# Loads two chunks ahead, a third residual tile and tokens weighted in place in the stage of pooled product and backward states

## The chip, the cores and the metric

The kernel runs on one core of one Trainium2 chip. The metric is the device time of one execution in microseconds. Five engines work side by side, each through its own queue in order: PE (TensorE, matrix products; its loading of weights is listed as PEld), DVE (VectorE), ACT (ScalarE), POOL (GpSimd) and SP (SyncE, which here only issues DMAs; ACT issues the stores).

## The reference, cut to what matters

One layer of a diffusion trunk over 2048 latent tokens of width 1024, with 256 context tokens as a prefix:

```
x   = LN(x; emb_ln_g, emb_ln_b);  h = x * (1 + sc1) + sh1
z, xbc, dt, up = split(h @ in_proj);  xbc = silu(conv5(xbc))
y   = SSD forward + SSD backward over chunks of 128 tokens
      (16 heads x 64, state 128; the scans start from the context's states)
y   = rms_norm((y + d_skip * xs) * silu(z)) * ssd_norm_g
p   = pool_mixer(up): box means of windows 2, 4, 8, 16 minus the token,
      one 256x256 map for each of four groups, times pool_scale
mix = concat(y, p) @ w_out
x   = LN(alpha * x + g1 * mix);   x = LN(alpha * x + g2 * swiglu(modulate(x)))
```

The backward state runs from the last chunk to the first: `h = h * decay + B^T (x * w_end)` for each chunk. The state before each chunk is needed later, in the forward scan.

## The kernel before, in words

All is fp32. Large products are made of three matmuls on split operands: each operand is a rounded high part (fp32r, by a cast on ACT) and a low part (by a subtraction), and `mm3` (L71 and on) adds high x high, high x low and low x high in one PSUM tile. Matmuls have a moving side of 512 columns, and L72 is the line of every one of them.

The stages, in order: normalisation and projections with the convolution; scores and pooling, which write the pooled differences `dp_d` to memory; the z blocks together with `pooled_weights`, which folds the pool maps, the pool scale, the gate g1 and the lower half of `w_out` into one operand W2 (high and low, W2H and W2L); then the stage of this change; then the forward scan with the output projection; then the feed-forward layer, which is over half of the time.

The stage of this change goes from chunk c = 15 down to c = 0 (NCH = 16 chunks of P = 128 tokens). For each chunk it does three things.

- The pooled product: `dp_d` of the chunk (two halves `dl` of 128x512, split into `dh` by a cast at L1053 and `dl` by a subtraction at L1054) times W2, in two halves of 512 columns with 24 matmuls each.
- The residual: the row block `x` (tile `bx`) is loaded, normalised with the statistics `stat` kept from the first stage (L1067, on DVE), multiplied by `ag` and added to `ab` (L1068 and L1069, on POOL); the product is added to it from PSUM (L1086, DVE), and the sum is stored in `base_d`.
- The backward state (c > 0): the state `hb` is stored; the chunk's tokens `xt` (1024 columns of x and 128 of B) are loaded, x is weighted per head into a tile `xs` (L1062, POOL), and `add_state` (L368 and on) decays the state on DVE (L371), makes two matmuls of 512 columns, which are issued as two instructions each, and adds them (L377, DVE).

Beside this, one block of 128 rows of the upper half of `w_out` in every second chunk becomes the operand of the later output projection: two halves are loaded into one tile `wyraw`, multiplied by the norm's gain and g1 (L1096, DVE), cast into WyH (L1097, ACT) and subtracted into WyL (L1098, DVE).

`prep(c - 1)` does the loads and splits of the next chunk in the iteration of c, ahead of c's product. Tiles with a number in their tag (`dh0`, `dl1`, `bx0`, `xt1`) exist once for each parity of c (`dh` and `dl` in two halves each), so a load of chunk c - 2 waits until chunk c has done with the tile.

Two pools hold the tiles: `bp` at the left takes the place of two of the operands of the z blocks that ended earlier; `b3` at the right lies where other operands of the z blocks lay. `after(t)` writes one element of a tile on POOL from `gate`, which is ready when the third group of pooled weights is split, so that the load behind it does not stand in SP's queue too early.

The order of each engine's queue is laid out when the program is built, by a scheduler that follows the text's order only among instructions which its own model of time has ready at once. So a queue's order isn't the text's: all sixteen loads of `wyraw` are issued by 986 us, in the first nine chunks, where the text spreads them over fifteen. Waits within a queue are then in order: an instruction that waits holds up all that stand behind it on its engine.

Of the kernel before, what the change touches and what calls it, by code (L numbers as in the profile page):

```python
# [8 lines left out]
F32 = mybir.dt.float32  # L9
F32R = mybir.dt.float32r  # L10
I32 = mybir.dt.int32
AF = mybir.ActivationFunctionType
ALU = mybir.AluOpType

P = 128
D = 1024
KB = D // P
T = 2048
NCH = T // P
TC = 256  # L20
NCC = TC // P
H = 16
# [13 lines left out]
def hybrid_block_kernel(ctx: ExitStack, tc: tile.TileContext, a: dict, out: bass.AP, dbg=None):  # L36
    nc = tc.nc
    mult, add, sub, amin = ALU.mult, ALU.add, ALU.subtract, ALU.min
# [11 lines left out]
    def pool(name, side="left"):  # L50
        return tc.tile_pool(name=name, bufs=1, side=side, reuse_waits="tile")
# [10 lines left out]
    def load(dst, src):  # L62
        nc.sync.dma_start(dst, src)

    def store(dst, src):
        nc.scalar.dma_start(dst, src)

    def f32(ap):
        return ap.bitcast(F32)
# [4 lines left out]
    def mm3(ps, lh, ll, rh, rl, nk, tick=None):  # L74
        for k in range(nk):
            mm(ps, lh(k), rh(k), k == 0, False)
            mm(ps, lh(k), rl(k), False, False)
            mm(ps, ll(k), rh(k), False, k == nk - 1)
            if tick is not None:
                tick(k)  # L80
# [58 lines left out]
    xbc_d = dram.tile([T, D + P], F32, name="xbc_d")  # L139
    bt_d = dram.tile([P, T], F32, name="bt_d")  # L140
    ct_d = dram.tile([P, T], F32, name="ct_d")
    dp_d = dram.tile([D, T], F32, name="dp_d")
    sz_d = dram.tile([D, T], F32, name="sz_d")
    w_d = dram.tile([NCH, P, H * P], F32, name="w_d")
    base_d = dram.tile([T, D], F32, name="base_d")
    hb_d = dram.tile([NCH * P, D], F32, name="hb_d")
# [61 lines left out]
    stat = cst.tile([P, NCH, 2], F32, name="stat")  # L208
# [6 lines left out]
    def ln_h(src, t0, r, tp, parts, o, keep):  # L215

        st = small.tile([P, 2, 2, 6], F32, tag="st", name="st")
        mv = small.tile([P, 2, 2], F32, tag="mv", name="mv")
        ve = small.tile([P, 2], F32, tag="ve", name="ve")
        xs = []  # L220
        for i in range(2):
            x = tp.tile([P, D], F32, tag="lnx", name="lnx", bufs=6)
            if keep and t0 < 3 * 256:
                nc.gpsimd.tensor_copy(x[:, 0:1], mod_gate)
            load(x, src[t0 + i * P:t0 + (i + 1) * P, :])
            xs.append(x)
        yield
        for i in range(2):
            ln_stats(xs[i], st[:, i], mv[:, i])
        nc.vector.tensor_scalar(out=ve, in0=mv[:, :, 1], scalar1=EPS, scalar2=None, op0=add)  # L230
        rs = rsqrt(ve, 2, "rs")
        nm = small.tile([P, 2], F32, tag="nm", name="nm")
        nc.vector.tensor_scalar(out=nm, in0=mv[:, :, 0], scalar1=-1.0, scalar2=None, op0=mult)
        if keep:
            c0 = t0 // P
            nc.gpsimd.tensor_scalar(out=stat[:, c0:c0 + 2, 0], in0=nm, scalar1=1.0, scalar2=0.0, op0=mult, op1=add)
            nc.gpsimd.tensor_scalar(out=stat[:, c0:c0 + 2, 1], in0=rs, scalar1=1.0, scalar2=0.0, op0=mult, op1=add)
        for i in range(2):
            nc.gpsimd.tensor_scalar(out=xs[i], in0=xs[i], scalar1=nm[:, i:i + 1], scalar2=rs[:, i:i + 1], op0=add, op1=mult)
        yield  # L240
        w = slice(o, o + 256)
        HT, LT = parts()
        for k in range(KB):
            pt = ps_tr()
            for i in range(2):
                nc.tensor.transpose(pt[:, i * P:(i + 1) * P], xs[i][:, k * P:(k + 1) * P], ident)  # L246
            h = tp.tile([P, 256], F32, tag="h32", name="h32", bufs=3)
            if k % 4 == 1:
                nc.vector.tensor_scalar(out=h, in0=pt[:, 0:256], scalar1=modA[:, r, k:k + 1], scalar2=modB[:, r, k:k + 1], op0=mult, op1=add)
            else:  # L250
                nc.scalar.activation(out=h, in_=pt[:, 0:256], func=AF.Identity, scale=modA[:, r, k:k + 1], bias=modB[:, r, k:k + 1])
            nc.scalar.copy(HT[:, k, w], h)
            e = nc.vector if k % 4 == 3 else nc.gpsimd
            e.tensor_tensor(out=LT[:, k, w], in0=h, in1=f32(HT[:, k, w]), op=sub)
            yield
# [106 lines left out]
    def heads(ap):  # L362
        return ap.rearrange("p (h d) -> p h d", d=HD)

    def bch(ap, n=H, m=HD):
        return ap.unsqueeze(2).broadcast_to([P, n, m])

    def add_state(hn, hp, dec, xw, bt):  # L368

        if hp is not None:  # L370
            nc.vector.tensor_tensor(out=heads(hn), in0=heads(hp), in1=bch(dec), op=mult)  # L371
        for g in range(2):
            ps = ps_ss()
            s = slice(g * 512, (g + 1) * 512)
            mm(ps, bt, xw[:, s], True, True)
            if hp is not None:
                nc.vector.tensor_tensor(out=hn[:, s], in0=hn[:, s], in1=ps, op=add)  # L377
            else:
                nc.vector.tensor_copy(hn[:, s], ps)


    x_in = a["x"].rearrange("o t d -> (o t) d")
# [57 lines left out]
    class Ahead:  # L440

        gens = [None] * 8
        at, n = 0, 0
# [467 lines left out]
    w_out = a["w_out"].rearrange("o (k p) n -> p (o k) n", p=P)  # L911
# [105 lines left out]
    eac, wend, cdec = (coef[:, i] for i in range(3))  # L1017
# [10 lines left out]
    bp = sb.enter_context(pool("b2"))  # L1028
# [4 lines left out]
    def after(t):  # L1033
        nc.gpsimd.tensor_copy(t[:, 0:1], gate)
# [7 lines left out]
    hb = b3.tile([P, D], F32, tag="hb1", name="hb")  # L1042
    after(hb)
    load(hb, hb0)
    def prep(c):
        rows_c = slice(c * P, (c + 1) * P)
        dh, dl = [], []
        for q in range(2):
            dh.append((b3 if c % 2 else bp).tile([P, 4, P], F32R, tag=f"dh{c % 2}", name="dh", bufs=2))
            dl.append((b3 if c % 2 else bp).tile([P, 4, P], F32R, tag=f"dl{c % 2}", name="dl", bufs=2))  # L1050
            d = f32(dl[q])
            load(d, dp_d[q * 512:(q + 1) * 512, rows_c].rearrange("(k p) t -> p k t", p=P))
            nc.scalar.copy(dh[q], d)  # L1053
            nc.vector.tensor_tensor(out=dl[q], in0=d, in1=f32(dh[q]), op=sub)  # L1054
        xs = xt = None
        if c > 0:
            xt = b3.tile([P, D + P], F32, tag=f"xt{c % 2}", name="xt")
            if c >= NCH - 2:
                after(xt)
            load(xt, xbc_d[rows_c, :])  # L1060
            xs = b3.tile([P, D], F32, tag=f"xs{c % 2}", name="xs")
            nc.gpsimd.tensor_tensor(out=heads(xs), in0=heads(xt[:, 0:D]), in1=bch(wend[:, c, H:2 * H]), op=mult)  # L1062
        x = (b3 if c % 2 else bp).tile([P, D], F32, tag=f"bx{c % 2}", name="bx")
        if c >= NCH - 2:
            after(x)
        load(x, x_in[rows_c, :])
        nc.vector.tensor_scalar(out=x, in0=x, scalar1=stat[:, c, 0:1], scalar2=stat[:, c, 1:2], op0=add, op1=mult)  # L1067
        nc.gpsimd.tensor_tensor(out=x, in0=x, in1=ag, op=mult)  # L1068
        nc.gpsimd.tensor_tensor(out=x, in0=x, in1=ab, op=add)  # L1069
        return xs, xt, dh, dl, x  # L1070

    cur = prep(NCH - 1)
    for c in range(NCH - 1, -1, -1):
        rows_c = slice(c * P, (c + 1) * P)
        xs, xt, dh, dl, x = cur
        if c > 0:
            store(hb_d[rows_c, :], hb)
            hn = (b3 if c % 2 == 0 else sr).tile([P, D], F32, tag=f"hb{(c - 1) % 2}", name="hb")
            add_state(hn, hb, cdec[:, c, H:2 * H], xs, xt[:, D:D + P])
            hb = hn  # L1080
            cur = prep(c - 1)
        for nh in range(2):
            n = slice(nh * 512, (nh + 1) * 512)
            ps = ps_mm()
            mm3(ps, lambda k: dh[k // 4][:, k % 4, :], lambda k: dl[k // 4][:, k % 4, :], lambda k: W2H[k][:, n], lambda k: W2L[k][:, n], KB)
            nc.vector.tensor_tensor(out=x[:, n], in0=x[:, n], in1=ps, op=add)  # L1086
        store(base_d[rows_c, :], x)
        if c % 2 == 1:
            k = (NCH - 1 - c) // 2
            for nh in range(2):  # L1090
                n = slice(nh * 512, (nh + 1) * 512)
                raw = b3.tile([P, 512], F32, tag="wyraw", name="wyraw")
                if c == NCH - 1 and nh == 0:
                    after(raw)
                load(raw, w_out[:, k, n])
                nc.vector.scalar_tensor_tensor(out=raw, in0=raw, scalar=v_ng[:, k:k + 1], in1=g1b[:, n], op0=mult, op1=mult)  # L1096
                nc.scalar.copy(WyH[k][:, n], raw)  # L1097
                nc.vector.tensor_tensor(out=WyL[k][:, n], in0=raw, in1=f32(WyH[k][:, n]), op=sub)  # L1098
        if c == 1:
            bo.close()  # L1100
            se = sx.enter_context(pool("se", "right"))
    sb.close()
    ph1.close()

# [544 lines left out]
```

## Time and profile before

| | us |
|---|---|
| median of three runs | 2763.98 (2759.65 to 2764.54) |
| the profiled execution | 2764.45 |
| its span | 2762.7 |
| PE busy | 2649.9 (96%) |
| DVE busy | 1767.3 (64%) |
| POOL busy | 1371.5 (50%) |
| ACT busy | 913.3 (33%) |

Times in the trace count from the start of the span. Busy time is the time in which an engine had an instruction at work. Matmuls overlap in the profile, so the busy time of a group of matmuls is more than the time it takes; their pace is read from the chain of waits, where each piece begins where the one before ends. An arrow names what released a waiting instruction; where it waited for several things it names the last. Some matmul records are missing from a trace.

### The profile page before, as it was taken

The page shows a single profiled execution, that of the slowest core. Times are in us where ns is not written, and L with a number is a line of the kernel's source. Part 1 is how long each engine was busy: PE and PEld are TensorE (multiplying, and loading weights), DVE is VectorE, ACT ScalarE, POOL GpSimd, SP SyncE. Part 2 cuts the span into 40 slices and gives each one's busy share as a digit, 9 for nine tenths or more (in the row PEclk, how much of TensorE's full clock was granted, in tenths as well). Part 3 has the DMA queues.
Part 4 walks back from the last instruction along what each step waited for, and adds up shares of the span by engine and source line. Part 5 has one row for each costly group of instructions (what it writes and reads, how often), then busy time and mean ns, then how long its engine had stood idle before and what let it go on. Part 6 is the DMA issues. An engine that isn't in the chain of part 4 may idle for free.

```text
span 2762.7 us, 33705 instructions
## 1 busy us (share of the span) xinstructions
PE 2649.9 (96%) x11778; PEld 2053.4 (74%) x11778; DVE 1767.3 (64%) x2209; ACT 913.3 (33%) x1611; POOL 1371.5 (50%) x1166
## 2 busy tenths in 40 slices
PE   7989999999999899999989999999999998999997
PEld 4557788778877666777768888877888887888776
DVE  4748745864646675677786777777765555545763
ACT  3544332116532111343352332233323323333332
POOL 5654322433435454556554565555555543315467
PEclk9989999999999999999999999999999999999998
DMA  9822321226756566667664455564433327545643
GB/s 325 263 73 71 112 77 45 69 97 181 197 163 221 186 219 234 200 227 250 209 230 163 158 180 169 170 217 146 164 96 103 103 84 238 156 148 175 208 148 109
DMA packets 392449, 454.86 MB, mean 165 GB/s; under 512 B 31173, under 2 KB 287920, under 8 KB 388952
## 3 DMA queue, kind: packets, MB, share of 16 engines
q1 hardware_dynamic: 298016, 340.29, 39.7%
q10 hardware_dynamic: 93784, 112.30, 11.3%
q8 instruction: 93, 1.52, 0.2%
q0 software_dynamic: 480, 0.11, 0.1%
q14 instruction: 76, 0.62, 0.1%
HBM read 294.34 MB, written 158.28 MB: 164 GB/s over the span
## 4 chain that ended last, share of the span: by engine, by line
PE 80%; DMA 6%; DVE 5%; POOL 3%; issue 3%; ACT 2%; SPq 0%; ACTq 0%; POOLq 0%; DVEq 0%
PE b L72 42%; PE mm L72 30%; PE ss L72 6%; DVE cv L359 1%; DMA wada<-in_w_ada 1%; POOL acc L1530 1%; DMA base_d<-bx 1%; POOL acc L1529 1%; PE tr L1161 1%; PE tr L604 1%; PE tr L246 0%; DMA dl<-dp_d 0%; DMA lnx<-in_x 0%; DMA bx<-in_x 0%; PE tr L1211 0%
## 5 line engine op out<-in xcount | busy, mean ns | idle before, releaser
L72 PE MATMUL b<-wd,h 128*128 128x512 f32 x1848 | 433.9, 397 | 13.4 <-ACT h L1355 7.4
L72 PEld LDWEIGHTS b<-wd,h 128*128 128x128 f32 x1848 | 349.5, 190 | 97.6 <-DVE wd L1344 8.0
L72 PE MATMUL mm<-HT,wh 128*128 128x512 f32 x832 | 332.1, 402 | 2.8 <-ACT u L906 2.3
L72 PE MATMUL mm<-LT,wh 128*128 128x512 f32 x832 | 332.5, 400 | 0.0
L72 PE MATMUL mm<-HT,wl 128*128 128x512 f32 x832 | 331.1, 399 | 0.0
L1329 DVE TENSOR_TENSOR ev<-ev,b 128x512 f32<-128x512 f32 x301 | 200.8, 680 | 135.6 <-PE b L72 120.3
L1316 POOL TENSOR_TENSOR x<-cs,x 128x512 fp32r<-128x512 f32 x132 | 185.7, 1407 | 172.3 <-ACT x L1315 158.5
L1356 DVE TENSOR_TENSOR h<-h 128x768 fp32r<-128x768 f32 x112 | 125.8, 1131 | 155.0 <-ACT h L1355 154.8
L72 PEld LDWEIGHTS mm<-HT,wh 128*128 128x128 f32 x832 | 158.1, 190 | 40.2 <-ACT u L906 3.1
L72 PEld LDWEIGHTS mm<-LT,wh 128*128 128x128 f32 x832 | 157.6, 189 | 36.4 <-issue 0.6
L72 PEld LDWEIGHTS mm<-HT,wl 128*128 128x128 f32 x832 | 157.4, 189 | 36.5 <-issue 0.6
L359 DVE SCALAR_TENSOR_TENSOR cv<-raw,vt,cv 128x512 f32<-128x512 f32 (+2 forms) x160 | 134.0, 848 | 59.6 <-POOL cv L357 53.8
L1315 ACT CAST x<-cs 128x512 fp32r<-128x512 f32 x176 | 108.8, 622 | 182.0 <-PE b L72 80.2
L1316 POOL TENSOR_TENSOR x<-wraw,x 128x512 fp32r<-128x512 f32 x44 | 63.3, 1439 | 190.8 <-ACT x L1315 140.6
L1355 ACT CAST h<-h 128x768 fp32r<-128x768 f32 x112 | 87.0, 782 | 212.0 <-DMA h<-hid_d 185.2
L1315 ACT CAST x<-wraw 128x512 fp32r<-128x512 f32 x132 | 80.1, 620 | 201.1 <-PE b L72 100.6
L267 POOL TENSOR_TENSOR wl<-wraw,wh 128x1024 fp32r<-128x1024 f32 (+1 forms) x35 | 83.4, 2382 | 116.7 <-ACT wh L264 116.7
L72 PE MATMUL b<-y1h,x 128*128 128x512 f32 x344 | 115.1, 396 | 4.1 <-ACT y1h L1275 4.1
L72 PE MATMUL mm<-WyH,yh 128*128 128x512 f32 x256 | 115.6, 451 | 1.9 <-ACT yh L1172 1.9
L72 PE MATMUL b<-y0h,x 128*128 128x512 f32 x344 | 115.3, 396 | 1.9 <-DVE ev L1329 1.9
L72 PE MATMUL b<-y4h,x 128*128 128x512 f32 x344 | 115.5, 397 | 0.0
L72 PE MATMUL b<-y3h,x 128*128 128x512 f32 x344 | 115.1, 395 | 0.0
(412 smaller groups left out, 6315.8 us busy)
## 6 DMA issues: line engine op xcount, KB each, us to landing
wraw<-in_w_gate SPq DMA_DIRECT2D x44, 512.0 KB
wraw<-in_w_up SPq DMA_DIRECT2D x44, 512.0 KB
hid_d<-ev ACTq DMA_DIRECT2D x88, 256.0 KB
h<-hid_d SPq DMA_DIRECT2D x56, 384.0 KB
tw_d<-wdr SPq DMA_DIRECT2D x77, 256.0 KB
wd<-tw_d SPq DMA_DIRECT2D x77, 256.0 KB
wada<-in_w_ada SPq DMA_DIRECT2D x72, 256.0 KB
wraw<-in_in_proj SPq DMA_DIRECT2D x35, 512.0 KB
```

Source lines behind the costliest of these rows:

```text
L72: nc.tensor.matmul(ps, lhsT=lhsT, rhs=rhs, start=start, stop=stop)
L267: nc.gpsimd.tensor_tensor(out=wl[:, split:], in0=raw[:, split:], in1=f32(wh[:, split:]), op=sub)
L359: nc.vector.scalar_tensor_tensor(out=dst, in0=raw[:, d:d + n], scalar=w(d), in1=dst, op0=mult, op1=add)
L604: nc.tensor.transpose(pt[0:n, i * P:(i + 1) * P], cv[:, j0 + i * P:j0 + i * P + n], ident)
L1161: nc.tensor.transpose(pt[:, q * P:(q + 1) * P], t[:, pr * P:(pr + 1) * P], ident)
L1315: nc.scalar.copy(h, src)
L1316: (nc.vector if i % 3 == 0 else nc.gpsimd).tensor_tensor(out=l, in0=src, in1=f32(h), op=sub)
L1329: nc.vector.tensor_tensor(out=o, in0=t, in1=ps, op=add)
L1355: nc.scalar.copy(th, f32(tl))
L1356: nc.vector.tensor_tensor(out=tl, in0=f32(tl), in1=f32(th), op=sub)
L1529: e.tensor_tensor(out=x, in0=x, in1=bvec["ln2_g"][:, m], op=mult)
L1530: e.tensor_tensor(out=x, in0=x, in1=bvec["ln2_b"][:, m], op=add)
```

## The change

The diff touches the statistics of the first normalisation and the whole loop of the stage.

- `stat` holds the product of the negative mean and the reciprocal deviation in place of the negative mean, so that the normalisation of the residual is one activation, `scale * x + bias`; it moves from DVE to ACT.
- The loads are split off: `fetch_d`, `fetch_t`, `fetch_x` and `fetch_wy`. Those of chunk c - 2 are issued in the iteration of c, behind its product, in the order tokens, `w_out`, residual, pooled differences. `split(c - 1)` does the casts, subtractions and weighting, ahead of c's product.
- The residual has three tiles by c modulo 3 in place of two by parity. `wyraw` has two tiles in place of one, and the two halves of a block are loaded together, two chunks ahead.
- The tokens are weighted in place in `xt`; the two tiles `xs` go.
- Both casts of a chunk are issued ahead of both subtractions.
- The store of `base_d` is issued in the next iteration, behind that one's `split`. The store of the state and `add_state` stand behind the first half of the product.
- The subtraction that makes WyL moves from DVE to POOL.

```diff
-            nc.gpsimd.tensor_scalar(out=stat[:, c0:c0 + 2, 0], in0=nm, scalar1=1.0, scalar2=0.0, op0=mult, op1=add)
+            nc.gpsimd.tensor_tensor(out=stat[:, c0:c0 + 2, 0], in0=nm, in1=rs, op=mult)
...
-    def prep(c):
-        rows_c = slice(c * P, (c + 1) * P)
-        dh, dl = [], []
+    def of(c):
+        return b3 if c % 2 else bp
+
+    def fetch_d(c):
+        dl = []
         for q in range(2):
...
+            dl.append(of(c).tile([P, 4, P], F32R, tag=f"dl{c % 2}", name="dl", bufs=2))
+            load(f32(dl[q]), dp_d[q * 512:(q + 1) * 512, c * P:(c + 1) * P].rearrange("(k p) t -> p k t", p=P))
+        return dl
+
+    def fetch_t(c):
+        if c == 0:
+            return None
+        xt = b3.tile([P, D + P], F32, tag=f"xt{c % 2}", name="xt")
+        if c >= NCH - 2:
+            after(xt)
+        load(xt, xbc_d[c * P:(c + 1) * P, :])
+        return xt
+
+    def fetch_x(c):
+        x = (b3 if c % 3 else bp).tile([P, D], F32, tag=f"bx{c % 3}", name="bx")
+        if c >= NCH - 3:
+            after(x)
+        load(x, x_in[c * P:(c + 1) * P, :])
+        return x
+
+    def fetch_wy(k):
+        raws = []
+        for nh in range(2):
+            raws.append(b3.tile([P, 512], F32, tag="wyraw", name="wyraw", bufs=2))
+            if k == 0:
+                after(raws[nh])
+            load(raws[nh], w_out[:, k, nh * 512:(nh + 1) * 512])
+        return raws
+
+    def split(c, dl, xt, x):
+
+        dh = []
+        for q in range(2):
+            dh.append(of(c).tile([P, 4, P], F32R, tag=f"dh{c % 2}", name="dh", bufs=2))
+            nc.scalar.copy(dh[q], f32(dl[q]))
+        for q in range(2):
+            nc.vector.tensor_tensor(out=dl[q], in0=f32(dl[q]), in1=f32(dh[q]), op=sub)
         if c > 0:
...
-            nc.gpsimd.tensor_tensor(out=heads(xs), in0=heads(xt[:, 0:D]), in1=bch(wend[:, c, H:2 * H]), op=mult)
...
-        nc.vector.tensor_scalar(out=x, in0=x, scalar1=stat[:, c, 0:1], scalar2=stat[:, c, 1:2], op0=add, op1=mult)
+            nc.gpsimd.tensor_tensor(out=heads(xt[:, 0:D]), in0=heads(xt[:, 0:D]), in1=bch(wend[:, c, H:2 * H]), op=mult)
+        nc.scalar.activation(out=x, in_=x, func=AF.Identity, scale=stat[:, c, 1:2], bias=stat[:, c, 0:1])
         nc.gpsimd.tensor_tensor(out=x, in0=x, in1=ag, op=mult)
         nc.gpsimd.tensor_tensor(out=x, in0=x, in1=ab, op=add)
...
+    last = NCH - 1
+    got = {last: (fetch_d(last), fetch_t(last), fetch_x(last))}
+    wy = fetch_wy(0)
+    got[last - 1] = fetch_d(last - 1), fetch_t(last - 1), fetch_x(last - 1)
+    dh = split(last, *got[last])
+    stored = None
+    for c in range(last, -1, -1):
         rows_c = slice(c * P, (c + 1) * P)
...
+        dl, xt, x = got.pop(c)
+        nxt = split(c - 1, *got[c - 1]) if c else None
+        if stored:
+            store(*stored)
         for nh in range(2):
             n = slice(nh * 512, (nh + 1) * 512)
             ps = ps_mm()
             mm3(ps, lambda k: dh[k // 4][:, k % 4, :], lambda k: dl[k // 4][:, k % 4, :], lambda k: W2H[k][:, n], lambda k: W2L[k][:, n], KB)
+            if nh == 0 and c:
+                store(hb_d[rows_c, :], hb)
+                hn = (b3 if c % 2 == 0 else sr).tile([P, D], F32, tag=f"hb{(c - 1) % 2}", name="hb")
+                add_state(hn, hb, cdec[:, c, H:2 * H], xt[:, 0:D], xt[:, D:D + P])
+                hb = hn
             nc.vector.tensor_tensor(out=x[:, n], in0=x[:, n], in1=ps, op=add)
-        store(base_d[rows_c, :], x)
+        stored = base_d[rows_c, :], x
+        wr, wy = wy, None
+        if c > 1:
+            xt = fetch_t(c - 2)
+            if c % 2 == 0:
+                wy = fetch_wy((NCH - c) // 2)
+            x = fetch_x(c - 2)
+            got[c - 2] = fetch_d(c - 2), xt, x
         if c % 2 == 1:
...
                 nc.vector.scalar_tensor_tensor(out=raw, in0=raw, scalar=v_ng[:, k:k + 1], in1=g1b[:, n], op0=mult, op1=mult)
                 nc.scalar.copy(WyH[k][:, n], raw)
-                nc.vector.tensor_tensor(out=WyL[k][:, n], in0=raw, in1=f32(WyH[k][:, n]), op=sub)
+                nc.gpsimd.tensor_tensor(out=WyL[k][:, n], in0=raw, in1=f32(WyH[k][:, n]), op=sub)
+        dh = nxt
...
+    store(*stored)
```

## Rows read from the trace of the kernel before

**Rows 1.** The page's head and the part on PE.
```profile
span 2762.7 us, 33705 instructions
PE 2649.9 (96%) x11778; PEld 2053.4 (74%) x11778; DVE 1767.3 (64%) x2209; ACT 913.3 (33%) x1611; POOL 1371.5 (50%) x1166
```

**Rows 2.** By stretch: length, PE, PEld, DVE, ACT, POOL busy, PEclk, DMA share, GB/s.
```profile
849.45:991.72 142.27, 124.87 (x473) 92.59 (x474) 99.87 (x102) 19.61 (x34) 63.61 (x27) 0.93 0.60 200
991.72:1078.43 86.71, 86.71 (x357) 67.42 (x357) 59.67 (x54) 7.46 (x12) 51.15 (x20) 0.99 0.63 211
```

**Rows 3.** The chain of waits in the stage: start, duration, what.
```profile
849.45 13.47 PE mm L72 x50
...
899.31 7.30 DMA base_d<-bx
...
906.74 4.08 DMA bx<-in_x
...
1003.49 1.72 PE ss L72 x4
1005.21 11.20 PE mm L72 x48
...
1018.12 10.94 PE mm L72 x48
```

**Rows 4.** Who waited for whom in the stage: total, times, longest.
```profile
ACT WyH L1097 <- DVE wyraw L1096: 77.7, 10, 10.2
ACT dh L1053 <- DMA dl<-dp_d: 53.6, 11, 8.4
...
PE ss L72 <- DVE hb L377: 17.4, 5, 6.1
DVE wyraw L1096 <- DMA wyraw<-in_w_out: 12.3, 8, 2.6
...
PE mm L72 <- ACT dh L1053: 2.8, 1, 2.8
```

**Rows 5.** DVE's groups by line, first half: busy, mean, idle before.
```profile
L1098 DVE TENSOR_TENSOR WyL<-wyraw,WyH 128x512 fp32r<-128x512 f32 x15 | 23.6, 1574 | 5.5 <-ACT WyH L1097 5.5
L1054 DVE TENSOR_TENSOR dl<-dl,dh 128x512 fp32r<-128x512 f32 x18 | 20.0, 1111 | 3.8 <-ACT dh L1053 3.6
L1096 DVE SCALAR_TENSOR_TENSOR wyraw<-wyraw,vt,g1b 128x512 f32<-128x512 f32 x16 | 17.9, 1119 | 12.3 <-DMA wyraw<-in_w_out 12.3
L371 DVE TENSOR_TENSOR hb<-hb,coef 128x1024 f32<-128x1024 f32 x10 | 14.3, 1427 | 0.4 <-DMA hb<-hb 0.3
L377 DVE TENSOR_TENSOR hb<-hb,ss 128x512 f32<-128x512 f32 x18 | 11.9, 676 | 0.2 <-PE ss L72 0.2
...
L1067 DVE TENSOR_SCALAR bx<-bx,stat 128x1024 f32<-128x1024 f32 x8 | 6.9, 866 | 23.1 <-DMA bx<-in_x 23.1
```

**Rows 6.** Groups by line, whole span: two shapes that the change adds.
```profile
L1173 POOL TENSOR_TENSOR yl<-y,yh 128x512 fp32r<-128x512 f32 x32 | 44.8, 1406 | 0.0
...
L1131 ACT ACTIVATE sz<-sz 128x1024 f32<-128x1024 f32 x16 | 16.9, 1057 | 24.4 <-DMA sz<-sz_d 24.4
```

**Rows 7.** Single lines in the stage: nanoseconds, shortest, median and longest.
```profile
L1062 POOL TENSOR_TENSOR xs<-xt,coef x15: 1902/2356/2988, 853.1 to 1037.2; 128x1024 f32<-128x1024 f32 x15
...
L1054 DVE TENSOR_TENSOR dl<-dl,dh x30: 676/693/2834, 849.4 to 1061.3; 128x512 fp32r<-128x512 f32 x30
...
L371 DVE TENSOR_TENSOR hb<-hb,coef x15: 1210/1227/2923, 851.7 to 1048.0; 128x1024 f32<-128x1024 f32 x15
...
L1096 DVE SCALAR_TENSOR_TENSOR wyraw<-wyraw,vt,g1b x16: 737/752/2877, 858.2 to 989.5; 128x512 f32<-128x512 f32 x16
...
L377 DVE TENSOR_TENSOR hb<-hb,ss x30: 673/674/686, 863.8 to 1060.7; 128x512 f32<-128x512 f32 x30
```

**Rows 8.** Timeline ahead of the stage: a cast and a matmul that waited.
```profile
819.10 0.62 ACT L1053 CAST dh<-dl 128x512 fp32r<-128x512 f32 x1 [4.96 <-DMA dl<-dp_d]
...
821.32 0.50 PE L72 MATMUL mm<-w2rh,pwh 128*128 128x512 f32 x1 [3.17 <-DVE W2L L958]
```

More of the change, by code (lines that the diff above doesn't have):

```diff
@@ L1044, in hybrid_block_kernel @@
     load(hb, hb0)
-    def prep(c):
-        rows_c = slice(c * P, (c + 1) * P)
-        dh, dl = [], []
+    def of(c):
+        return b3 if c % 2 else bp
+    def fetch_d(c):
+        dl = []
         for q in range(2):
[L1049 to L1055, printed above, removed]
-        if c > 0:
[L1057 to L1061, printed above, removed]
-            nc.gpsimd.tensor_tensor(out=heads(xs), in0=heads(xt[:, 0:D]), in1=bch(wend[:, c, H:2 * H]), op=mult)
[L1063 to L1066, printed above, removed]
-        nc.vector.tensor_scalar(out=x, in0=x, scalar1=stat[:, c, 0:1], scalar2=stat[:, c, 1:2], op0=add, op1=mult)
@@ L1068, in prep @@
         nc.gpsimd.tensor_tensor(out=x, in0=x, in1=ag, op=mult)
         nc.gpsimd.tensor_tensor(out=x, in0=x, in1=ab, op=add)
-        return xs, xt, dh, dl, x
-    cur = prep(NCH - 1)
-    for c in range(NCH - 1, -1, -1):
-        rows_c = slice(c * P, (c + 1) * P)
[L1075 to L1081, printed above, removed]
+        return dh
@@ L1085, in hybrid_block_kernel @@
             mm3(ps, lambda k: dh[k // 4][:, k % 4, :], lambda k: dl[k // 4][:, k % 4, :], lambda k: W2H[k][:, n], lambda k: W2L[k][:, n], KB)
-            nc.vector.tensor_tensor(out=x[:, n], in0=x[:, n], in1=ps, op=add)
-        store(base_d[rows_c, :], x)
+            if nh == 0 and c:
[3 more added lines that the diff above has]
+                hb = hn
+            nc.vector.tensor_tensor(out=x[:, n], in0=x[:, n], in1=ps, op=add)
+        stored = base_d[rows_c, :], x
[6 more added lines that the diff above has]
+            got[c - 2] = fetch_d(c - 2), xt, x
         if c % 2 == 1:
-            k = (NCH - 1 - c) // 2
-            for nh in range(2):
+            k = (last - c) // 2
+            for nh, raw in enumerate(wr):
                 n = slice(nh * 512, (nh + 1) * 512)
[L1092 to L1095, printed above, removed]
                 nc.vector.scalar_tensor_tensor(out=raw, in0=raw, scalar=v_ng[:, k:k + 1], in1=g1b[:, n], op0=mult, op1=mult)
                 nc.scalar.copy(WyH[k][:, n], raw)
-                nc.vector.tensor_tensor(out=WyL[k][:, n], in0=raw, in1=f32(WyH[k][:, n]), op=sub)
+                nc.gpsimd.tensor_tensor(out=WyL[k][:, n], in0=raw, in1=f32(WyH[k][:, n]), op=sub)
+        dh = nxt
         if c == 1:
```

## The prediction

> **What bounds the kernel now.** I read the page first: TensorE is busy for 96% of the span [rows 1], so a change can win only where PE stands, and there is little of that. Next the table by stage [rows 2], cut at the first pooled matmul (849.45 us) and the last (1078.43): the stage that the change touches lasts 229.0 us. It falls into two halves. From 991.72 on PE is busy for all of 86.71 us; before that it is busy for 124.87 of 142.27 us, at a mean granted clock of 0.93, so partly at 1.2 GHz, the lower of its two levels (the other is 2.4).
>
> The chain of waits tells what the stage would take if PE never stood. A chunk is 48 matmuls (10.94 or 11.20 us, mean 11.07) and one backward state (1.72) [rows 3]. The second half holds seven chunks (c = 6 to 0) and five states: 7 x 11.07 + 5 x 1.72 = 86.1 us against 86.71. The first half holds nine chunks (c = 15 to 7) and ten states: 9 x 11.07 + 10 x 1.72 = 116.8 us against 142.27. So 25.4 us are lost in the first half, and that is what the change can reach in this stage. Of these, 17.4 are stalls in front of the state's matmuls, each put down to the addition at L377 on DVE [rows 4]; the rest is matmuls at the lower clock. The first chunk, at the slow start, takes 13.47 us for 50 matmuls where 50 / 48 x 11.07 = 11.5 would do: 2.0 us of the loss, there whatever is changed.
>
> Why is L377 late? Its own time is 0.68 us. It stands in DVE's queue behind others, so I added up DVE over the first half: busy 99.87 us [rows 2], and idle 23.1 before L1067 (the residual's load), 12.3 before L1096 (the w_out load), 5.5 before L1098 (the cast on ACT), 3.8 before L1054 and under 1 elsewhere [rows 5]. Together 144.6, which is the half's length: DVE in its order is the bound there, not PE. The chain shows the same [rows 3]: store of the residual tile (7.30 us), its reload (4.08), then DVE's work in order. With two residual tiles a load must wait for a store just issued. In the second half there is no w_out work, and PE is full.
>
> **The change part by part.**
>
> *The residual's scaling goes from DVE (L1067) to ACT.* DVE loses 6.9 us busy and the 23.1 us of waiting. ACT gains one activation of 128x1024 a chunk; L1131 has that shape at 1.057 us [rows 6], so 9.5 us in the first half, beside ACT's 19.61 of 142.27: hidden. The wait for the load goes to ACT, and queued behind it there are the casts of the next chunk and the stores. With a third tile the load follows a store that is a chunk old (12.8 us against the 7.30 the store took), so I cost the wait at nothing; with that cover gone it is the 23.1 us again, on ACT.
>
> *The subtraction for WyL goes from DVE (L1098) to POOL.* DVE loses 23.6 us busy and the 5.5 us wait for the cast. POOL gains 16 x 1.406 = 22.5 us, by L1173, the same operation in the same shape [rows 6]. POOL's 63.61 us [rows 2] become 86.1 of a half that would last 116.8: hidden, as far as throughput goes.
> The Trainium skill speaks against this move: "GPSIMD Engine Reference", section 4.1 Engine selection, gives elementwise work on a tile to VectorE, with GpSimd about twice as slow for two inputs. This trace agrees for DVE undisturbed (the same subtraction at L1054 takes 0.676 us at best [rows 7]) but not in place, where L1098's mean is 1.574 us [rows 5] against POOL's 1.406. By the page's factor on DVE's mean the 16 would take POOL 50 us, which with 63.61 is 114, still inside 116.8.
>
> *The state's tokens are weighted in place.* The same multiplication (L1062) writes back into its own tile; two tiles go. The token tile was already held until the state's matmuls, which read the other part of it, so nothing is freed later. Cost 0. Bounds: the POOL multiplication has been 1.90 to 2.99 us [rows 7], so 15 of them cannot move POOL by more than 15 x 1.1 = 16 us either way, and POOL has 30.7 to spare.
>
> *Loads two chunks ahead, two w_out tiles, another order.* The operand tiles dh and dl are still two pairs deep, so a load cannot start before the product two chunks back has read its tile, as before. What the order can change is which loads stand in front in SP's queue; each load waits there for its tile, and all behind it wait too. The w_out halves: DVE's 12.3 us before L1096 could vanish with the second tile, or stay; I leave all of it in. The first chunk's operands still wait for the last z block, and PE for their cast (2.8 us [rows 4]); earlier PE stood 3.17 us behind ACT's queue, where a cast for chunk 14 had waited 4.96 us for its load [rows 8]. The new ACT activation could add such a wait or the new order take it away: -3.2 to +3.2 us, and -2.8 to 0 for the first; I take 0 for both.
>
> *The state moved behind the first half of the product, the store of base deferred.* Same instructions, and the store still precedes the need by a chunk. PE's sum is the same; the state's inputs get 5.5 us more slack. Cost 0, between -5 and +5 (one stall of the kind in [rows 4], longest 6.1).
>
> *The product of mean and deviation in the statistics (L236)*: one tiny POOL operation for another, 0.
>
> *Sum.* DVE in the first half: 99.87 - 6.9 - 23.6 = 69.4 us busy, plus 12.3 + 3.8 still waiting = 85.5. If each new POOL operation holds up a DVE one for its whole length, 85.5 + 22.5 = 108. Both lie under PE's 116.8, so PE becomes the bound again. I leave 5 us of stalls (two of the longest w_out wait, 2.6 us [rows 4]), between 0 and all 17.4. Gain: 25.4 - 2.0 - 5.0 = 18.4 us. From the profiled execution's 2764.45 us (span 2762.7 plus 1.75 around it) that is 2746.0; the median shown is 0.5 lower, so 2746 either way. What follows starts earlier by the same amount: the scan of the first chunk waits for the tiles of chunks 1 and 0, which come free at the same distance from the stage's end.
>
> **The rivals.**
>
> *DVE stays the bound, through POOL.* DVE operations with two SBUF inputs stretch when POOL works: L1054 ranges from 0.676 to 2.834 us, L371 from 1.21 to 2.92, L1096 from 0.737 to 2.877, while L377, with one input in PSUM, stays between 0.673 and 0.686 [rows 7]. POOL will be busier. If all 18 + 10 + 16 of them in the first half took their longest, they would need 51.0 + 29.2 + 46.0 = 126 us instead of 52.2 [rows 5]: 74 us more. With two in three, 85.5 + 49 = 135 us: a gain of only 7 us, 2757. Against it: the second half, with POOL busy for 59% of the time (45% in the first), has PE full.
> The Trainium skill has this as a rule ("GPSIMD Engine Reference", section 8 Key points: SBUF interfaces shared with VectorE, contention for DVE instructions with two SBUF inputs or in a two-port mode); by that rule, and the trace agrees, this rival cannot be dismissed.
>
> *Nothing gained.* The waits move from DVE to ACT: casts stand behind the activation that waits for the residual's load, and the dl subtraction behind the casts. 2764. For it: ACT's casts already waited for loads, 53.6 us [rows 4]. Against it: the third tile.
>
> *Slower: POOL stands in its queue.* WyL on POOL waits for the cast, that for L1096, that for the load; behind it on POOL are the weighting of the tokens and the two residual steps, for which PE waits. ACT stood 77.7 us before its cast for L1096 [rows 4], 4.86 us for each of 16. POOL has 116.8 - 63.6 = 53.2 us free; 16 x (1.406 + 4.86) = 100.3 is 47.1 too many, more than the 25.4 that can be won: +21.7, 2786. It decides from a standing time of 3.5 us: 16 x (1.406 + 3.5) = 78.5 = 53.2 + 25.4. Against it: ACT had nothing else to do meanwhile, and two w_out tiles let loads run ahead.
>
> **How the numbers follow.** Chances: PE-bound again 0.52 (own range 2741 to 2752), DVE stays the bound 0.20, nothing gained 0.14, slower 0.14. Range: the low end takes all 25.4 + 3.2, 2736; the high end takes in the second rival and the third, 2766, and leaves the slow one out. A measurement of this kernel tells 0.2% (5.5 us) from no change. Faster: 0.52 + 0.20 = 0.72, its edge near 2758.5 lying just beyond the second rival; same 0.14; slower 0.14.
>
> **What would show it.** Right: in the stage's first half no idle time of PE before the state's matmuls, chunks 12.8 us apart from the second on, a clock near 1.00, no DVE instruction waiting for a residual's load, and a stage of 205 to 213 us. DVE the bound: L1054, L1096 and L371 near 2.8 us and PE waiting for L377 as now. POOL: long idle times in front of WyL, and PE waiting for the weighted tokens. Wrong altogether: the stage shorter and the stages behind it longer by as much.

## The result, and the profile after

| | before | changed |
|---|---|---|
| median, us | 2761.82 (4 runs, 2754.72 to 2764.54) | 2739.83 (4 runs, 2736.07 to 2742.18) |
| profiled execution, us | 2764.45 | 2742.18 |
| the stage, first to last pooled matmul, us | 228.98 | 210.63 |

The ratio is 0.9922, with a 95% interval of 0.9906 to 0.9938: 22.0 us faster, 17 to 26 by the interval. 2746 was forecast (range 2736 to 2766), a gain of 18.4 us, with the stage at 205 to 213 us.

The stage by stretches, cut at 940.08 us, where PE stops standing and 15 of the 16 w_out halves are done (columns as in [rows 2]):

```profile
849.97:940.08 90.11, 85.64 (x337) 64.03 (x338) 71.12 (x57) 24.57 (x34) 73.66 (x35) 0.98 0.69 235
940.08:1060.60 120.52, 120.52 (x493) 92.38 (x493) 67.11 (x67) 21.77 (x27) 63.97 (x28) 1.00 0.65 218
```

The chain of waits in the stage, as in [rows 3]:

```profile
849.97 11.85 PE mm L72 x50
...
874.74 4.66 DMA base_d<-bx
...
892.83 2.25 POOL WyL L1131
...
926.09 4.29 DMA dl<-dp_d
...
941.79 11.07 PE mm L72 x48
952.87 1.72 PE ss L72 x4
...
1044.12 16.48 PE mm L72 x72
```

From 941.79 on the chain is PE alone, chunk after chunk at 11.07 and 1.72 us, for nine and a half chunks where it was seven before. The first six and a half take 90.11 us; 6.5 x 11.07 + 6 x 1.72 = 82.3 would do. So 7.8 us are still lost, where the prediction left 7.0; in 4.3 of them PE stood (6.0 us below, less the 1.7 ahead of the stage's first matmul), the rest is matmuls at less than the full pace (the granted clock is 0.83, so partly the lower level of 1.2 GHz, from 930 to 940 us, and 1.00 in the other slices of 10 us from 850 to 950). Who waited for whom, as in [rows 4]:

```profile
ACT bx L1090 <- DMA bx<-in_x: 49.8, 10, 7.6
...
DVE wyraw L1129 <- DMA wyraw<-in_w_out: 9.9, 5, 4.4
...
PE mm L72 <- DVE dl L1087: 3.2, 2, 2.3
...
PE mm L72 <- ACT dh L1085: 1.7, 1, 1.7
...
PE mm L72 <- ACT WyH L1130: 1.1, 1, 1.1
```

The wait for the residual's load is there in full, 49.8 us, but on ACT, and little of it reaches PE. The 17.4 us before the state's matmuls are gone. DVE's groups in the first stretch, as in [rows 5], are longer beside a POOL that is busy for 82% of the time, where it was 45%:

```profile
L1129 DVE SCALAR_TENSOR_TENSOR wyraw<-wyraw,vt,g1b 128x512 f32<-128x512 f32 x15 | 27.8, 1864 | 11.2 <-DMA wyraw<-in_w_out 8.9 <-POOL bx L1092 2.3
...
L1087 DVE TENSOR_TENSOR dl<-dl,dh 128x512 fp32r<-128x512 f32 x12 | 19.2, 1622 | 3.0 <-ACT dh L1085 2.9
...
L371 DVE TENSOR_TENSOR hb<-hb,coef 128x1024 f32<-128x1024 f32 x6 | 10.4, 1735 | 1.3 <-DMA dl<-dp_d 1.1
```

The means have risen from 1.119, 1.111 and 1.427 us: 15 x 0.745 + 12 x 0.511 + 6 x 0.308 = 19.2 us of DVE's time. Single instructions of the changed kernel between 849 and 992 us tie this to POOL: the `dl` subtractions with POOL idle for over 90% of their length took 0.678 to 0.693 us (4 of them), those with POOL busy for over 90% of it 1.89 in the mean (15), and the 41 additions with one input in PSUM (L377, L1116) 0.673 to 0.689, whatever POOL did. But the 19.2 us are not all the price of WyL on POOL: o_raw below adds no work to POOL and has means of 1.602, 1.603 and 1.558 us (850 to 990 us, POOL busy for 55%).

Of the 22.3 us between the two profiled executions, 18.35 are the stage. It began 0.5 later, and 4.5 came behind it, 3.2 of these in the gate and up part of the feed-forward (from its first y0 product to its last: 831.4 us before, 828.2 after). Over the fourteen kernels here that part took 826.9 to 831.5 us without following the stage, so I count those 3 us as scatter.

### The profile page after: what moved, and what is told of

The parts are those of the page before. It is cut to its first block, busy times and chain, and to the rows that moved or that the text cites. A ratio compares the mean times of both kernels' runs of the same rounds, so it can differ in the third digit from the quotient of the medians.

```text
span 2740.4 us, 33709 instructions
## 1 busy us (share of the span) xinstructions
PE 2641.8 (96%) x11778; PEld 2046.5 (75%) x11778; DVE 1740.7 (64%) x2177; ACT 935.5 (34%) x1627; POOL 1398.8 (51%) x1184
## 4 chain that ended last, share of the span: by engine, by line
PE 77%; DMA 7%; DVE 6%; POOL 4%; issue 3%; ACT 2%; SPq 0%; ACTq 0%; POOLq 0%; DVEq 0%
PE b L72 40%; PE mm L72 29%; PE ss L72 6%; DVE cv L359 2%; DMA h<-hid_d 1%; DMA wada<-in_w_ada 1%; POOL acc L1565 1%; POOL acc L1564 1%; PE tr L1196 1%; DMA dl<-dp_d 1%; PE tr L1246 0%; POOL WyL L1131 0%; PE tr L246 0%; SPq L63 0%; DVE wd L1379 0%
```

## The experiments

Each was timed in five rounds beside the kernel before on the same chip, in three sets (before: medians 2766.09, 2761.73 and 2762.30). "Stage" is from the first to the last start of the matmuls on W2's low part in the one profiled execution; "scan" is from there to the first y0 product of the feed-forward. The row of the changed kernel is the result above, measured apart from the three sets.

| kernel | ratio (95%) | stage | scan |
|---|---|---|---|
| before | 1 | 228.0 | 372.5 |
| changed | 0.9922 (0.9906 to 0.9938) | 209.7 | 371.1 |
| u_wyl: changed, WyL on DVE | 0.9952 (0.9934 to 0.9970) | 220.8 | 372.0 |
| u_scale: changed, scaling on DVE | 0.9928 (0.9911 to 0.9945) | 211.4 | 372.0 |
| u_tile: changed, two residual tiles | 0.9907 (0.9889 to 0.9926) | 205.1 | 371.3 |
| u_ahead: changed, loads one chunk ahead | 0.9915 (0.9897 to 0.9934) | 204.4 | 372.5 |
| u_raw1: u_ahead with one w_out tile | 0.9941 (0.9928 to 0.9954) | 216.0 | 373.0 |
| o_wyl: before, WyL on POOL | 0.9958 (0.9942 to 0.9974) | 218.5 | 371.4 |
| o_scale: before, scaling on ACT | 1.0015 (1.0005 to 1.0026) | 233.5 | 370.6 |
| o_tile: before, third residual tile, tokens in place | 1.0007 (0.9997 to 1.0017) | 232.4 | 369.7 |
| o_raw: before, two w_out tiles, tokens in place | 0.9944 (0.9930 to 0.9958) | 216.2 | 369.8 |
| o_wyl_raw: both, tokens in place | 0.9932 (0.9919 to 0.9945) | 209.3 | 369.3 |
| v_pace: changed, w_out paced | 0.9910 (0.9897 to 0.9924) | 202.1 | 370.5 |
| o_pace: before, w_out paced | 1.0004 (0.9995 to 1.0013) | 217.7 | 383.4 |

### Undoing one part of the change

**u_wyl**

```diff
-nc.gpsimd.tensor_tensor(out=WyL[k][:, n], in0=raw, in1=f32(WyH[k][:, n]), op=sub)
+nc.vector.tensor_tensor(out=WyL[k][:, n], in0=raw, in1=f32(WyH[k][:, n]), op=sub)
```

> The changed kernel with the subtraction for WyL back on DVE; all else as changed. Theory (the queue of DVE, in its order, bounds the first half of the stage): DVE gets back 23.6 us of work and the 5.5 us of waiting for the cast, 85.5 + 29.1 = 114.6 us for the first half, just under PE's 116.8 and with no room for anything out of step; the stage takes 216 to 224 us in place of 210.6, the whole 0.994 to 0.997 of before. Rival (the third residual tile alone did it): as the changed kernel, 0.992, stage near 210. Rival (the order of the loads in the text did it): 0.992 as well.

The stage took 220.8 us, the whole 0.9952: as the theory had it. The subtraction's place is worth 11 us of the stage.

**u_scale**

```diff
-nc.scalar.activation(out=x, in_=x, func=AF.Identity, scale=stat[:, c, 1:2], bias=stat[:, c, 0:1])
+nc.vector.tensor_scalar(out=x, in0=x, scalar1=stat[:, c, 1:2], scalar2=stat[:, c, 0:1], op0=mult, op1=add)
```

> The changed kernel with the residual's scaling back on DVE (multiply and add with the new statistics). Theory: DVE gets 13 us more work in the stage, and waits for residual loads again, but short ones, since each load has a free tile; 85.5 + 7 + a few us stays under 116.8: stage 211 to 217 us, 0.992 to 0.995 of before. Rival (moving the scaling off DVE is what counts, because of the wait): stage near 225, 0.998. Rival (third tile alone): as changed, 0.992.

211.4 us and 0.9928: within the theory's range, and hardly a loss. DVE waited 9.5 us for residual loads in the stage, where before it was 36.4.

**u_tile**

```diff
-        x = (b3 if c % 3 else bp).tile([P, D], F32, tag=f"bx{c % 3}", name="bx")
-        if c >= NCH - 3:
+        x = (b3 if c % 2 else bp).tile([P, D], F32, tag=f"bx{c % 2}", name="bx")
+        if c >= NCH - 2:
```

> The changed kernel with two residual tiles by parity in place of three. Theory: the wait for store and reload (23 us in the first half) is back, but on ACT, where casts of the next chunk stand behind it; part of it reaches PE: stage 213 to 220 us, 0.993 to 0.996 of before. Rival (third tile alone did it): back to before, stage 225 to 229, 0.999 to 1.001.

Both were wrong: 205.1 us and 0.9907, no loss at all. The third tile does nothing here that the times can tell.

**u_ahead**

```diff
-    wy = fetch_wy(0)
-    got[last - 1] = fetch_d(last - 1), fetch_t(last - 1), fetch_x(last - 1)
     dh = split(last, *got[last])
...
+        if c:
+            got[c - 1] = fetch_d(c - 1), fetch_t(c - 1), fetch_x(c - 1)
         nxt = split(c - 1, *got[c - 1]) if c else None
...
-        if c > 1:
-            xt = fetch_t(c - 2)
...
-            got[c - 2] = fetch_d(c - 2), xt, x
         if c % 2 == 1:
             k = (last - c) // 2
-            for nh, raw in enumerate(wr):
+            for nh, raw in enumerate(fetch_wy(k)):
```

> The changed kernel with its loads one chunk ahead, right ahead of the split, and the w_out block loaded where it is used, as the text had it before; three tiles, two w_out tiles, in place, ACT and POOL as changed. Theory: the scheduler lays out nearly the same queue, because a load goes out as soon as its tile is free: stage 209 to 213 us, 0.991 to 0.994 of before, no difference from the changed kernel. Rival (loads two chunks ahead in the text did it): stage above 220, 0.996 to 1.000.

0.9915, no difference from the changed kernel that can be told; the stage, at 204.4 us, was shorter than expected by 4.6. The lead in the text brings nothing: the built queue of SP issues the loads in nearly the same order with and without it (the last w_out load goes out at 933.5 us, in the changed kernel at 937.0).

So two parts that were to carry the gain by the theory, the scaling and the third tile, could each be undone at little or no cost. The next set did single parts alone.

### One part alone, on the kernel before

**o_wyl** (the edit of u_wyl the other way round, at L1098)

```diff
-nc.vector.tensor_tensor(out=WyL[k][:, n], in0=raw, in1=f32(WyH[k][:, n]), op=sub)
+nc.gpsimd.tensor_tensor(out=WyL[k][:, n], in0=raw, in1=f32(WyH[k][:, n]), op=sub)
```

> The kernel before with one part alone: the subtraction for WyL on POOL. Theory (DVE's queue bounds the first half): 144.6 - 23.6 - 5.5 = 115.5 us for DVE, and up to 22.5 more where POOL holds up DVE; stage 212 to 222 us where before it took 229.0 and changed 210.6; 0.993 to 0.998 of before, more than half of the whole gain. Rival (each part alone gives nothing, because the wait for the residual's load stays in DVE's queue): stage 226 or more, 0.999 to 1.001.

218.5 us and 0.9958: the theory's range, half of the whole gain.

**o_scale**

```diff
-nc.gpsimd.tensor_scalar(out=stat[:, c0:c0 + 2, 0], in0=nm, scalar1=1.0, scalar2=0.0, op0=mult, op1=add)
+nc.gpsimd.tensor_tensor(out=stat[:, c0:c0 + 2, 0], in0=nm, in1=rs, op=mult)
...
-nc.vector.tensor_scalar(out=x, in0=x, scalar1=stat[:, c, 0:1], scalar2=stat[:, c, 1:2], op0=add, op1=mult)
+nc.scalar.activation(out=x, in_=x, func=AF.Identity, scale=stat[:, c, 1:2], bias=stat[:, c, 0:1])
```

> The kernel before with one part alone: the residual's scaling on ACT, with the statistics for it; two residual tiles, all else as before. Theory: 144.6 - 6.9 - 23.1 = 114.6 us for DVE; stage 212 to 222 us, 0.993 to 0.998 of before. Rival (the wait only moves to ACT, and through its casts to DVE's subtractions): stage 226 or more, 0.999 to 1.001.

The theory fell: the stage is longer, 233.5 us, the whole 1.0015. DVE no longer waits for residual loads, and waits for w_out loads instead. Its group by line in the first half, where that wait was 12.3 us [rows 5]:

```profile
L1096 DVE SCALAR_TENSOR_TENSOR wyraw<-wyraw,vt,g1b 128x512 f32<-128x512 f32 x15 | 18.6, 1237 | 44.8 <-DMA wyraw<-in_w_out 39.7 <-DMA dl<-dp_d 5.1
```

The reason is in SP's own waits, which the prediction does not use. Here they are for the kernel before, between 850 and 990 us (who waited for whom: total, times, longest):

```profile
SPq L63 <- DVE WyL L1098: 61.7, 12, 8.0
SPq L63 <- DMA base_d<-bx: 39.0, 7, 7.8
SPq L63 <- PE mm L72: 12.8, 3, 6.7
```

SP stood for 100.7 of 140 us, for the subtraction that frees the w_out tile and for the store that frees the residual tile, and all loads queued behind stood too (12.8 us more it stood for PE). And for o_scale:

```profile
SPq L63 <- DVE WyL L1098: 55.8, 10, 8.5
SPq L63 <- DMA base_d<-bx: 51.1, 7, 7.9
```

The residual's load still stands at the head of SP's queue until the store has landed, and the next w_out load behind it. o_scale's chain shows one turn (start, duration, what): the subtraction lets a w_out load go, DVE works on, the sum is stored, and only then SP issues the residual's load (946.76) and behind it the next w_out load.

```profile
926.43 2.32 DVE WyL L1098
928.77 3.41 DMA wyraw<-in_w_out
...
932.27 2.32 DVE wyraw L1096
...
938.00 0.61 DVE bx L1086
...
938.68 7.94 DMA base_d<-bx
...
946.76 0.33 SPq L63
...
947.19 4.24 DMA wyraw<-in_w_out
```

The wait on DVE was for the queue, not for one load; with the one taken away DVE stood at the next.

**o_tile** (with the tokens weighted in place, for room)

```diff
-        x = (b3 if c % 2 else bp).tile([P, D], F32, tag=f"bx{c % 2}", name="bx")
-        if c >= NCH - 2:
+        x = (b3 if c % 3 else bp).tile([P, D], F32, tag=f"bx{c % 3}", name="bx")
+        if c >= NCH - 3:
...
-            xs = b3.tile([P, D], F32, tag=f"xs{c % 2}", name="xs")
+            xs = xt[:, 0:D]
```

> The kernel before with a third residual tile, and the tokens weighted in place, which makes the room for it; scaling and WyL stay on DVE. With the changed kernel two tiles did as well as three, because the wait stood on ACT. Theory: here the wait stands on DVE, and the third tile shortens it: 144.6 less most of 23.1, about 125: stage 213 to 222 us, 0.993 to 0.998 of before. Rival (DVE waits for the load itself and not for the store ahead of it): stage 225 to 229, 0.998 to 1.001.

232.4 us and 1.0007: the theory fell again. SP's waits say why:

```profile
SPq L63 <- DVE WyL L1098: 58.3, 10, 8.6
SPq L63 <- DMA base_d<-bx: 40.5, 6, 7.9
```

SP waits for the store as long as with two tiles (39.0). The scheduler issues a load as soon as its own model has the tile free; a third tile moves the load forward by a chunk, and it stands at the head of the queue behind a store again: the sixth load goes out at 912.9 us, 7.9 behind the store of the third block (905.0). Its use on DVE has moved forward with it, to 28 us ahead of the addition that needs it (916.9 and 945.3 us), and DVE waits for it as before, 25.4 us between 850 and 990. The rival's reason was not the right one either: it is the store that SP waits for.

**o_raw** (with the tokens in place)

```diff
-raw = b3.tile([P, 512], F32, tag="wyraw", name="wyraw")
-if c == NCH - 1 and nh == 0:
+raw = b3.tile([P, 512], F32, tag="wyraw", name="wyraw", bufs=2)
+if c == NCH - 1:
```

> The kernel before with two w_out tiles in place of one (and tokens weighted in place). Theory now: in the first half two queues turn in a ring. SP stands for the WyL subtraction that frees the w_out tile and for the store that frees the residual tile; DVE stands for the loads queued behind. The scaling alone on ACT only moved DVE's wait from the residual (23 us) to w_out (45). A second w_out tile loosens the first link, DVE's work stays: stage 218 to 228 us, 0.995 to 1.000 of before. Rival (DVE's work alone is the bound): 228 or more, 1.000.

0.9944, and 216.2 us: more than I expected, and as much as WyL on POOL. SP's wait for the subtraction is down from 61.7 to 32.7 us:

```profile
SPq L63 <- DMA base_d<-bx: 52.2, 8, 12.4
SPq L63 <- DVE WyL L1098: 32.7, 12, 6.9
```

DVE does all of its work here, 113.83 us busy in 140 (97.60 before). So DVE's work was not the bound by itself; its waits in a ring with SP were. The weighting in place is not what helped: o_tile has it too and gained nothing.

**o_wyl_raw** is o_wyl and o_raw together (with the tokens in place).

```diff
-nc.vector.tensor_tensor(out=WyL[k][:, n], in0=raw, in1=f32(WyH[k][:, n]), op=sub)
+nc.gpsimd.tensor_tensor(out=WyL[k][:, n], in0=raw, in1=f32(WyH[k][:, n]), op=sub)
...
-raw = b3.tile([P, 512], F32, tag="wyraw", name="wyraw")
-if c == NCH - 1 and nh == 0:
+raw = b3.tile([P, 512], F32, tag="wyraw", name="wyraw", bufs=2)
+if c == NCH - 1:
```

> The kernel before with WyL on POOL and two w_out tiles (and tokens in place); scaling on DVE, two residual tiles, the old text order. Theory (work off DVE, and SP's link loosened): stage 207 to 214 us, 0.991 to 0.994 of before, as much as the whole change. Rival (the scaling on ACT is needed as well): stage 216 to 222, like WyL alone, 0.995 to 0.997.

209.3 us, the stage of the whole change (209.7); the ratio of 0.9932 cannot be told from 0.9922. The theory as mended holds: these two edits, with the room that the weighting in place makes, are enough.

**u_raw1**

```diff
-            raws.append(b3.tile([P, 512], F32, tag="wyraw", name="wyraw", bufs=2))
+            raw = b3.tile([P, 512], F32, tag="wyraw", name="wyraw")
...
+            yield raw
```

> The kernel with all of the change but the two-chunk lead of the loads (that run took 204.4 us for the stage, 0.9915 of before), and here with one w_out tile, each half loaded at its use. Theory (SP's wait for the w_out tile is a link of the ring): stage 208 to 216 us, 0.992 to 0.996. Rival (the second tile does nothing once WyL is on POOL): as without it, stage 203 to 206, 0.991 to 0.992.

216.0 us against u_ahead's 204.4, and 0.9941: the theory's end of the range. With one w_out tile SP stands for it even where POOL does the subtraction:

```profile
SPq L63 <- POOL WyL L1124: 71.2, 13, 8.4
SPq L63 <- DMA base_d<-bx: 24.7, 5, 9.2
```

### Pacing the w_out work

**v_pace**

```diff
             if k == 0:
                 after(raws[nh])
+            else:
+                nc.vector.tensor_copy(raws[nh][:, 0:1], stored[1][:, 0:1])
```

> The changed kernel with the w_out loads paced: but for the first block, each load waits for a one-element copy on DVE out of the finished residual of the chunk in whose iteration it stands, so that one block goes through in every second chunk in place of one in each. Theory: what the changed kernel still loses (90.1 us for its first six and a half chunks, against 82.3) is DVE's work with two inputs held up by POOL while w_out is hurried through; spread out, 2 to 6 us of it come back: stage 204 to 208 us, 0.989 to 0.992 of before. Rival (the rest is the slow start and load waits): stage 209 to 212, 0.992 to 0.993. Against both: the pacing puts waiting w_out loads ahead of others in SP's queue, stage above 213.

202.1 us from start to start, below the theory's range and about the least that PE needs (15 x 12.79 + 11.07 = 202.9 by the chain's pieces, to the end of the last matmul); PE never stood. The ratio is 0.9910. The intervals of 0.9910 and 0.9922 overlap: the stage is shorter, and that the whole is faster than the changed kernel is not shown. Nor is it shown that the hurry with w_out, through POOL, is what the changed kernel still lost. DVE's operations with two SBUF inputs did not all get shorter (`dl`, `wyraw`, `hb` at L371, 850 to 990 us: 1.724, 2.164 and 1.386 us, in the changed kernel 1.673, 1.876 and 1.584). And u_tile and u_ahead, which hurry as the changed kernel does (all 16 halves multiplied by 990 us, here 12), have stages of 205.1 and 204.4 us: that leaves 2 to 3 of the 7.6 us for the pacing.

**o_pace**

```diff
                 if c == NCH - 1 and nh == 0:
                     after(raw)
+                elif c < NCH - 1:
+                    nc.vector.tensor_copy(raw[:, 0:1], x[:, 0:1])
```

> The kernel before with its w_out loads paced and nothing else changed: from the second block on, each load waits for a one-element copy on DVE out of the finished residual of the chunk it stands behind, so one block passes in two chunks in place of one in each. WyL and scaling stay on DVE, one w_out tile. Theory (the rate at which w_out is hurried through is what overfills the ring): DVE has 24 + 18 us of w_out work spread over sixteen chunks instead of nine; stage 206 to 214 us, 0.990 to 0.994 of before, as much as the whole change with none of its parts. Rival (the waits for store and reload of the residual bind by themselves): stage 220 or more, 0.997 to 1.003.

Neither: the stage went down by 10.3 us to 217.7, short of what the theory wanted, and the scan behind it became 10.9 us longer, so the whole is 1.0004. PE's waits at the start of the scan (1060 to 1090 us):

```profile
PE ss L72 <- POOL t L1138: 10.5, 1, 10.5
POOL t L1138 <- DMA xt<-xbc_d: 10.0, 1, 10.0
```

and SP's queue there (start, length, what):

```profile
1059.89 7.07 SPq L63 DMA_DIRECT2D wyraw<-in_w_out  x2
1067.06 0.38 SPq L63 DMA_DIRECT2D hf<-hf  x1
1067.53 0.56 SPq L63 DMA_DIRECT2D ctk<-ct_d  x1
1068.18 0.43 SPq L63 DMA_DIRECT2D xt<-xbc_d  x1
```

The last two w_out loads, held back to the end, stand in front of the scan's first loads: these go out about when they did before (`xt` at 1067.6 then, 1068.2 here), though the stage ended 12.9 us earlier. In v_pace, with two tiles, the last pair goes out from 1026.6 us on, 29 us ahead of the stage's end, and the scan keeps its 370.5.

## Why the prediction was right, and where its reasons were not

**The bound and its size: right.** 25.4 us to be won in the first half of the stage; 18.4 forecast, 18.35 measured in the stage of the profiled execution, and PE is the bound again from the seventh chunk on. The slow start of the first chunk, which I had left in (2.0 us), went: 11.85 us for 50 matmuls in place of 13.47, at a granted clock of 1.00 in place of 0.87. That the change did this is not shown. The stalls and slow stretches that took its place make 7.8 us, by the chain, against 7.0.

**WyL to POOL: right in its gain, too large in what DVE loses.** 9.5 us of the stage alone (o_wyl), 11.1 when undone (u_wyl). POOL had the time: 73.66 of 90.11 us busy. The subtractions took 1.591 us each there (15 in the first stretch), not 1.406. Over the stage as in the table (columns as in [rows 2]; before, o_wyl, o_scale, u_wyl, changed):

```profile
849.80:1077.80 228.00, 210.61 (x826) 159.17 (x825) 159.19 (x155) 26.73 (x46) 114.76 (x46) 0.96 0.61 203
847.80:1066.30 218.50, 208.08 (x827) 157.77 (x826) 148.10 (x139) 27.19 (x46) 133.94 (x62) 0.98 0.64 214
850.60:1084.10 233.50, 211.46 (x826) 159.01 (x825) 148.06 (x140) 44.63 (x61) 112.07 (x46) 0.95 0.60 201
851.40:1072.20 220.80, 208.86 (x826) 157.65 (x825) 141.26 (x140) 46.09 (x61) 109.08 (x46) 0.97 0.64 214
850.30:1060.00 209.70, 205.23 (x827) 155.60 (x826) 137.90 (x124) 46.00 (x61) 137.62 (x62) 0.99 0.67 226
```

DVE's busy time fell by 11.1 us with WyL alone on POOL, and by 3.4 between u_wyl and the changed kernel, where 23.6 were struck off: DVE's operations with two SBUF inputs grew longer beside POOL, within the 22.5 that I had as the upper bound. The mechanism of the rival "DVE stays the bound, through POOL" is thus at work; it did not win: DVE was idle for 19 of the first 90 us, and PE stood 3.2 us for it in the stage. The means of these operations are 0.3 to 0.75 us above those of the kernel before. The Trainium skill's "GPSIMD Engine Reference", section 8 Key points, has that contention, and the trace agrees. The scaling took as much off DVE (11.1 us, o_scale), and the stage got longer; so DVE's work alone does not decide. What sets the two apart is not shown by a run: the chain of the kernel before, from 845 to 1082 us, has 5.7 us of WyL in it and 1.9 of the scaling.

**The scaling to ACT: wrong.** The step failed where it said that DVE loses "6.9 us busy and the 23.1 us of waiting". Alone, it loses the work and keeps the waiting, now for w_out (39.7 us in place of 12.3), because the w_out loads stand in SP's queue behind the residual load that waits for a store: the stage gets 5.5 us longer (o_scale). In the changed kernel it is worth 1.7 us of the stage, and nothing that the times can tell (u_scale).

**The third tile as the cover for ACT's wait: wrong.** I costed that wait at nothing because a load would follow a store that is a chunk old. In the changed kernel the sixth load goes out at 902.4 us, 5.6 behind the store of the block whose tile it takes (896.8), and SP waits for stores longer than the 39.0 us of before (850 to 990 us):

```profile
SPq L63 <- DMA base_d<-bx: 46.1, 7, 8.9
```

The wait on ACT hurts little all the same: PE stood 4.3 us behind the stage's first matmul, for all causes. Why it hurts so little, no run shows. Two tiles do as well (u_tile).

**The loads' order and the second w_out tile: undersized.** I left all of DVE's 12.3 us before L1096 in and gave the part no gain. The second tile is one of the two that carry the change: 11.8 us of the stage alone (o_raw), 11.6 when undone (u_raw1 against u_ahead). The lead of two chunks is worth nothing (u_ahead).

**The sum came out right with two errors in it.** The scaling was credited with 30.0 us of DVE's time and by itself brought nothing; the second tile was credited with nothing and carries about half. The number could not show either: once PE is the bound, the stage is PE's own sum and the 7.0 us left in for the first chunk and stalls, whatever took DVE out of the way. That 18.4 and 18.35 agree so closely is luck: u_tile and u_ahead, whose whole times cannot be told from the changed kernel's, have stages 5 us shorter. DVE's queue was summed as if its waits belonged to single instructions, which could be struck off with them. They belonged to a ring: DVE frees the w_out tile, SP issues the loads in order, DVE waits for these. What helped was what loosened a link, a second tile, or took work out from between two links, WyL on POOL; either alone gives half, both together all. For WyL the ring is argued and not shown: in o_wyl SP's two waits, 57.7 and 34.5 us, are little less than before.

**The other rivals.** POOL's in-order wait before WyL came to 10.0 us where 3.5 for each of 16 (56) would have decided for "slower". "Nothing gained" describes o_tile; o_scale came out 0.15% longer (1.0005 to 1.0026).

**One sign of being right that proves little.** PE stands no more before the state's matmuls, as forecast, but so it is in every kernel whose state stands behind the first half of the product, the slow u_wyl and u_raw1 too (0.8 us at most), while o_wyl_raw, with an equal stage and the old place, keeps 3.2 us. It tells of the state's place, not of DVE's queue.

Open: why u_tile and u_ahead have a stage 5 us shorter than the changed kernel. Where the 5 us lie can be read: by the busy times over the stage PE was idle for 4.5 us in the changed kernel, 2.3 in u_tile and 1.6 in u_ahead, and from 930 to 940 us the granted clock was 0.83 there and 1.00 in the other two. Their whole times do not separate, and each stage length is from one execution. In-place weighting and the state's place behind the first half of the product were not tried by themselves; the two edits of o_wyl_raw, with the weighting in place, leave nothing of the stage's length for the latter to explain.

## What to carry to other kernels

Read the waits of the queue that issues the loads before striking off a wait on the engine that uses them: an engine that waits for a load may be waiting for whatever stands ahead of that load, and moving the user to another engine may only move the wait, as here. A deeper buffer helped here where it let the queue's head move (the second w_out tile), and did nothing where the order was made by issuing each load as early as its tile allowed (the third residual tile). Work that is held back to be out of the way must not end up in front of the next stage's first loads.

## What the runs showed of the hardware that I had not expected

The stores of 512 KB in the chain of the kernel before took 7.3 to 7.9 us from issue until the load that waited for them could go, and their reloads 3.7 to 4.2. In the changed kernel's chain one store took 4.66 us; what makes the difference is not shown.

ACT's activation of 128x1024 with scale and bias taken from a tile took 1.242 us (L1090, mean of 7), where the SiLU of the same shape without them takes 1.057 [rows 6]: I had used the latter as its price. The two differ in their function as well.
